# A two-layer hybrid decoder: the second mixer's small products in pairs of heads at fixed places

## The chip, the cores and the metric

The kernel runs on one core of a Trainium2 chip. The metric is device time in microseconds (us), the median of several executions; lower is better. The engines are named as the profile names them: PE multiplies matrices (PEld is its loading of the stationary operand), DVE and ACT do elementwise work, POOL fills constants, SP issues the transfers from HBM.

## What is computed

Two layers on x of 256 tokens by 1024 channels in float32, each a token mixer and a gated ConvFFN, each normed, shifted, scaled and gated by modulations of a conditioning vector c. Layer 0 has a dilated attention, layer 1 the gated linear attention (GLA) that the change touches. Cut to layer 1's mixer, and to one batch:

```python
mod = silu(c) @ w_ada[i] + b_ada[i]              # six pieces of 1024: sh1, sc1, g1, sh2, sc2, g2
h = rmsnorm(x, norm_mix[i]) * (1.0 + sc1) + sh1
...
proj = h @ w_in                                  # q, k: 4 heads of 128; v, r: 4 heads of 256; glr: 16
gk = log_sigmoid(glr @ w_gate + b_gate) / 16     # cut into chunks of 64 tokens
bcum, blast = cumsum(gk), its last row in each chunk
q_t, k_t, k_d = q * exp(bcum), k * exp(-bcum), k * exp(blast - bcum)
A = where(causal, q_t @ k_t.T, 0)                # in each chunk
kv = k_d.T @ v                                   # in each chunk
s_prev = the sum of earlier chunks' kv, decayed by exp(blast) at each step
o = A @ v + q_t @ s_prev
o = rmsnorm(o, g_norm)                           # over a head's 256 channels
x = x + g1 * ((o * silu(r)) @ w_out)
```

## The kernel before

Activations lie with channels in the partitions: x and h are eight tiles (kt) of 128 channels by 256 tokens. Each large product is made three times from split numbers (`mm3`): a weight block is loaded into `raw`, ACT casts it to `whi` (L187), DVE makes `wlo`, the rest (L191), in two halves of 1024 columns each, and PE multiplies hhi by whi (L197), hlo by whi (L198) and hhi by wlo (L199). The third product of a block therefore needs wlo's half. The pool behind `raw` has four buffers, those behind `whi` and `wlo` three each; a load starts when its buffer is free. All weight loads stand in SP's queue.

A modulation chunk (`ada_chunk`, `next_ada`) is one load of 1 MB and, on DVE, two dots of 1024 columns with silu(c) (L160). The second layer's chunks are spread over the program; the projection at the end of a mixer (`project`) needs piece 2, and the ConvFFN behind it pieces 3 to 5. `shift_columns` copies a piece into tiles that a later product reads.

The builder orders the instructions of each engine by a simulated timeline of its own. `behind(...)` puts an instruction behind others in that order; without it, the order is the simulation's.

The mixer of layer 1, in the order of the code: `h` is normed; four blocks of value weights give v; `log_gates` makes the decays e_q, e_k, e_d for all heads. Then for each head:

- `states(hd)`: large products for its query and key (tile pqk; head 0's query was made early), on DVE k_d, q_t and k_t, then small products in plain float32: two transposes of k_d (tile kdt, L995), two scores (tile a, L1001), and after a copy by ACT (kdT) and a mask by DVE (a_t) three key-value products (tiles kv and kdt, L1011), from which ACT and DVE make the states st0 to st2 (L1016, L1018).
- `output(hd)` or `products(hd)`: ten small products into tile o (L1034, L1037), then a sum of squares (osq, oacc) and its mean by PE (tile ms, L209), Ln and Exp, and two products by DVE into on (L1051).

`gate(n)` has 48 large products (tile pr) for two of r's tiles each, from weights w_r_b. Gates 0 and 1 lay the first half of wlo behind the last keys (`low=turned_keys[1:]`). Gate 2 reads copies of h's first two tiles from other addresses (lv, `level_tiles`). The calls at the end of the stage stand as `states` 0 and 1, `output` 0, `states` 2, `output` 1, `states` 3, products 2, gate 0, three modulation chunks, products 3, the norms of 2 and 3, gate 1, a chunk, gates 2 and 3; but PE takes a small product where the simulated timeline has its inputs ready, between large products of the next head.

Of the kernel before, what the change touches and what calls it, by code (L numbers as in the profile page):

```python
# [13 lines left out]
F32R = mybir.dt.float32r  # L14
# [4 lines left out]
P = 128  # L19
D = 1024  # L20
# [37 lines left out]
def trunk(ctx: ExitStack, tc: tile.TileContext, I, out):  # L58
# [396 lines left out]
    def next_ada():  # L455
        if rest:
            ada_chunk(*rest.pop(0))
# [318 lines left out]
    early = project(I["w_out_a"], lambda kt: (o_hi[kt], o_lo[kt]), 0, 0, between)  # L776
# [96 lines left out]
    def gt(shape, name, dt=F32, bufs=1, tag=None):  # L873
        return gla.tile(shape, dt, tag=tag or name, name=name, bufs=bufs)
# [8 lines left out]
    keep = gt([P, (NH_B - 1) * T], "keep", tag="D1")  # L883
# [24 lines left out]

    def gates_of(first, n, glr):
        def new(name, tag, columns=n * T):  # L910
            return gt([P, columns], name, tag=f"{tag}{min(first, 1)}")

        nz = new("nz", "A")
        for i in range(n):
# [47 lines left out]
        nc.scalar.copy(v[t][:, 0:512], pv[t][0])  # L962
        nc.vector.tensor_copy(v[t][:, 512:D], pv[t][1])

    o_n = []
    turned_keys = []

    def states(hd):
        if hd == 0:
            w = split(I["w_qk_b"][0][:, KT * P :], KT * P)  # L970
            pk = bank("pqk", "p")[:, :T]
            pq = early_q
            for kt in range(KT):
                mm3(pk, parts(w, P * kt), h[kt], kt == 0, kt == KT - 1)
        else:
            w = split(I["w_qk_b"][hd], 2048)
            pqk = bank("pqk", "p")
            pq, pk = pqk[:, :T], pqk[:, T:]
            for kt in range(KT):
                mm3(pq, parts(w, 2 * P * kt), h[kt], kt == 0, False)  # L980
                mm3(pk, parts(w, 2 * P * kt + P), h[kt], False, kt == KT - 1)
        part = min(hd, 1)
        e_q, e_k, e_d, dec = gates[part]
        own = hd - PARTS[part][0]
        c = slice(T * own, T * own + T)
        q_t, k_t, k_d = (gt([P, T], nm, bufs=2) for nm in ("q_t", "k_t", "k_d"))
        nc.vector.tensor_tensor(k_d, pk, e_d[:, c], op=ALU.mult)
        nc.vector.scalar_tensor_tensor(q_t, pq, P ** -0.5, e_q[:, c], op0=ALU.mult, op1=ALU.mult)
        last_key = nc.vector.tensor_tensor(k_t, pk, e_k[:, c], op=ALU.mult)

        ps = bank("kdt", "t")
        kd = gt([P, T], "kdT", bufs=2)
        for t in range(2):
            c = slice(P * t, P * t + P)
            nc.tensor.transpose(ps[:, c], k_d[:, c], ident)  # L995
        turned_keys[:] = nc.scalar.copy(kd, ps[:, :T]), last_key

        pa = bank("a", "s")
        for t in range(2):
            c = slice(P * t, P * t + P)  # L1000
            mm(pa[:, c], k_t[:, c], q_t[:, c], start=True, stop=True)  # L1001
        a_t = gt([P, 2, P], "a_t", bufs=2)
        nc.gpsimd.memset(a_t, 0.0)
        nc.vector.copy_predicated(a_t, causal.bitcast(U32), pa[:, :T].rearrange("p (a b) -> p a b", a=2))
        vh = slice(T * hd, T * hd + T)
        st = []
        kv = bank("kv", "s")
        for n in range(3):
            t, r = n // 2, slice(CH * (n % 2), CH * (n % 2) + CH)
            d = (kv[:, :T], ps[:, T:], kv[:, T:])[n]  # L1010
            mm(d, kd[r, P * t : P * t + P], v[t][r, vh], start=True, stop=True)  # L1011
        for n in range(3):
            d = (kv[:, :T], ps[:, T:], kv[:, T:])[n]
            s = gt([P, T], f"st{n}", bufs=2)
            if n == 0:
                nc.scalar.copy(s, d)  # L1016
            else:
                nc.vector.scalar_tensor_tensor(s, st[-1], dec[:, 4 * own + n : 4 * own + n + 1], d,  # L1018
                                               op0=ALU.mult, op1=ALU.add)
            st.append(s)  # L1020
        return q_t, a_t, st

    last_o = [None]

    def output(hd, *state):
        normed_output(hd, products(hd, *state))

    def products(hd, q_t, a_t, st):
        po = bank("o", "s")
        for et in range(2):  # L1030
            ev = slice(T * hd + P * et, T * hd + P * et + P)
            for t in range(2):
                d = po[:, T * et + P * t : T * et + P * t + P]
                mm(d, v[t][:, ev], a_t[:, t, :], start=True, stop=False)  # L1034
                for n in range(2 * t, 2 * t + 2):
                    if n:
                        last_o[0] = mm(po[:, T * et + CH * n : T * et + CH * n + CH],  # L1037
                           st[n - 1][:, P * et : P * et + P], q_t[:, CH * n : CH * n + CH],
                           start=False, stop=(n % 2 == 1))
        return po  # L1040

    def normed_output(hd, po, after=()):
        sq = gt([P, 2 * T], "osq", bufs=1)
        nc.scalar.activation(sq, po, AF.Square)
        acc = gt([P, T], "oacc", bufs=1)
        nc.vector.tensor_tensor(acc, sq[:, 0:T], sq[:, T : 2 * T], op=ALU.add)
        with behind(*after):
            rr = rstd_of([acc], 256, "s")
        on = gt([P, 2, T], f"on{hd}")
        for et in range(2):  # L1050
            nc.vector.scalar_tensor_tensor(on[:, et, :], po[:, T * et : T * et + T], col(C_GN + et), rr,  # L1051
                                           op0=ALU.mult, op1=ALU.mult)
        o_n.append(on)

    r_g = []

    def level_tiles():

        tiles = []
        for tag in ("A0", "B0", "C0", "cs0"):  # L1060
            tiles.append(gt([P, T], "lv", F32R, tag=tag))
            with behind(turned_keys[0]):
                nc.scalar.copy(tiles[-1], h[len(tiles) // 3][1 - len(tiles) % 2])
        return tiles[0:2], tiles[2:4]

    def gate(n):
        level = level_tiles() if n == 2 else ()

        w = split(I["w_r_b"][n], 2048, **({} if n else dict(after=(turned_keys[:1], ()), low=turned_keys[1:])))
        pr = bank("pr", "p")  # L1070
        for kt in range(KT):
            for s in range(2):
                with behind(*((), last_o, norm_ops[:1], ())[n]):
                    mm3(pr[:, T * s : T * s + T], parts(w, 2 * P * kt + P * s),
                        level[kt] if n == 2 and kt < 2 else h[kt], kt == 0 and s == 0, kt == KT - 1 and s == 1)
        r = gt([P, (2, 3)[n % 2] * T], f"r{n}", tag=("r0", "C1", "r2", "cs1")[n])
        r_g.append(r[:, : 2 * T].rearrange("p (a b) -> p a b", a=2))
        pr = pr.rearrange("p (a b) -> p a b", a=2)
        if n < 2:
            nc.scalar.copy(r_g[-1], pr)  # L1080
        else:
            with behind(*norm_ops[1:]):
                nc.scalar.activation(r_g[-1], pr, AF.Silu)

    s0 = states(0)
    s1 = states(1)
    output(0, *s0)
    s2 = states(2)
    output(1, *s1)
    s3 = states(3)  # L1090
    po2 = products(2, *s2)
    gate(0)
    for _ in range(3):
        next_ada()
    po3 = products(3, *s3)
    normed_output(2, po2, last_o)
    normed_output(3, po3)
    gate(1)
    next_ada()
    for n in range(4):  # L1100

        if n > 1:
            gate(n)
        r = r_g[n]
        if n < 2:
            with behind(*norm_ops[1:]):
                nc.scalar.activation(r, r, AF.Silu)
        for et in range(2):
            i = 2 * n + et
            on = o_n[n][:, et, :]  # L1110
            nc.vector.tensor_tensor(on, on, r[:, et, :], op=ALU.mult)
            hi, lo = o[i]
            last_hi = nc.scalar.copy(hi, on)
            nc.vector.tensor_tensor(lo, on, hi.bitcast(F32), op=ALU.subtract)
    exp_ln_after(last_hi)
    early = project(I["w_out_b"], o.__getitem__, 1, 0)
    gl_pool.__exit__(None, None, None)

# [147 lines left out]
```

## Time and profile before

| | us |
|---|---|
| three runs, median (lowest to highest) | 772.94 (772.45 to 775.13) |
| the profiled execution, device time | 769.98 |
| its span, first to last instruction | 768.2 |
| PE busy in the span | 756.4 |
| layer 1's mixer on PE, from its first key product to the projection's first | 63.52 |

The mixer lies from 493.27 to 556.79 us of the span, the projection from there to 578.55. A row of the timeline gives start, duration, engine, line, operation, the tiles written and read, and in brackets how long the engine stood idle before it and who ended that. PE's products overlap, so the time one takes from the others is the distance from its start to the next start. A small float32 product appears as two rows or x2.

### The profile page before, as it was taken

The page shows a single profiled execution, that of the slowest core. Times are in us where ns is not written, and L with a number is a line of the kernel's source. Part 1 is how long each engine was busy: PE and PEld are TensorE (multiplying, and loading weights), DVE is VectorE, ACT ScalarE, POOL GpSimd, SP SyncE. Part 2 cuts the span into 40 slices and gives each one's busy share as a digit, 9 for nine tenths or more (in the row PEclk, how much of TensorE's full clock was granted, in tenths as well). Part 3 has the DMA queues.
Part 4 walks back from the last instruction along what each step waited for, and adds up shares of the span by engine and source line. Part 5 has one row for each costly group of instructions (what it writes and reads, how often), then busy time and mean ns, then how long its engine had stood idle before and what let it go on. Part 6 is the DMA issues. An engine that isn't in the chain of part 4 may idle for free.

```text
span 768.2 us, 15928 instructions
## 1 busy us (share of the span) xinstructions
PE 756.4 (98%) x6420; PEld 730.1 (95%) x6420; DVE 625.2 (81%) x1120; ACT 490.3 (64%) x964; POOL 12.3 (2%) x36
## 2 busy tenths in 40 slices
PE   9999999999999999999999999999999999999997
PEld 5999989999998999999999998898999999999997
DVE  6988886878878788999988868887567998899662
ACT  5566675665666578676766456736667766666552
POOL 0000000000000010000000000000010000000100
PEclk9999999999999999999999999999999999999999
DMA  9989778587787856876656976776254756565741
GB/s 346 388 307 334 255 297 292 200 331 251 276 309 253 297 200 233 279 232 230 221 184 228 334 254 241 289 274 226 79 191 165 232 207 210 177 203 206 259 153 55
DMA packets 36487, 186.29 MB, mean 243 GB/s; under 512 B 8444, under 2 KB 11004, under 8 KB 20286
## 3 DMA queue, kind: packets, MB, share of 16 engines
q1 hardware_dynamic: 36032, 184.84, 67.4%
q8 instruction: 50, 0.82, 0.4%
q10 hardware_dynamic: 382, 0.45, 0.2%
q14 instruction: 23, 0.19, 0.1%
HBM read 184.17 MB, written 1.10 MB: 241 GB/s over the span
## 4 chain that ended last, share of the span: by engine, by line
PE 68%; DMA 13%; DVE 13%; ACT 3%; issue 2%; SPq 0%; ACTq 0%; DVEq 0%
PE pab L199 10%; PE pab L197 10%; PE pab L198 10%; DMA raw<-in_wqk 6%; PE pd L197 5%; PE pd L199 5%; PE pd L198 5%; DVE wlo L191 5%; DMA ada_raw<-in_w_ada 4%; DMA raw<-in_wv 3%; DVE ada_raw L160 3%; PE py L197 2%; PE py L198 2%; PE py L199 2%; PE pv L197 2%
## 5 line engine op out<-in xcount | busy, mean ns | idle before, releaser
L191 DVE TENSOR_TENSOR wlo<-raw,whi 128x1024 fp32r<-128x1024 f32 (+2 forms) x258 | 273.3, 1093 | 60.0 <-ACT whi L187 58.9
L187 ACT CAST whi<-raw 128x1024 fp32r<-128x1024 f32 (+2 forms) x258 | 230.5, 942 | 116.3 <-PE pab L198 40.7
L199 PE MATMUL pab<-hhi,wlo 128*128 128x256 f32 x672 | 184.7, 276 | 0.0
L198 PE MATMUL pab<-hlo,whi 128*128 128x256 f32 x672 | 184.6, 276 | 0.0
L197 PE MATMUL pab<-hhi,whi 128*128 128x256 f32 x672 | 183.2, 277 | 0.0
L198 PEld LDWEIGHTS pab<-hlo,whi 128*128 128x128 f32 x672 | 126.0, 188 | 0.2
L199 PEld LDWEIGHTS pab<-hhi,wlo 128*128 128x128 f32 x672 | 126.2, 188 | 0.0
L197 PEld LDWEIGHTS pab<-hhi,whi 128*128 128x128 f32 x672 | 125.1, 188 | 0.1
L160 DVE CUSTOM_DVE_ANT_0 ada_raw<-ada_raw,c_bc 128x1024 f32<-128x1024 f32 x96 | 113.5, 1221 | 10.3 <-DMA ada_raw<-in_w_ada 10.2
L199 PE MATMUL pd<-ghi,wlo 128*128 128x256 f32 x352 | 97.1, 276 | 0.0
L198 PE MATMUL pd<-glo,whi 128*128 128x256 f32 x352 | 97.1, 276 | 0.0
L197 PE MATMUL pd<-ghi,whi 128*128 128x256 f32 x352 | 96.8, 276 | 0.0
L197 PE MATMUL pqk<-hhi,whi 128*128 128x256 f32 x328 | 92.3, 281 | 0.1
L199 PE MATMUL pqk<-hhi,wlo 128*128 128x256 f32 x328 | 91.3, 278 | 0.0
L198 PE MATMUL pqk<-hlo,whi 128*128 128x256 f32 x328 | 91.0, 277 | 0.0
L199 PEld LDWEIGHTS pd<-ghi,wlo 128*128 128x128 f32 x352 | 66.1, 188 | 0.0
L198 PEld LDWEIGHTS pd<-glo,whi 128*128 128x128 f32 x352 | 66.1, 188 | 0.0
L197 PEld LDWEIGHTS pd<-ghi,whi 128*128 128x128 f32 x352 | 65.9, 188 | 0.0
L197 PEld LDWEIGHTS pqk<-hhi,whi 128*128 128x128 f32 x328 | 61.7, 188 | 0.7 <-issue 0.3
L199 PEld LDWEIGHTS pqk<-hhi,wlo 128*128 128x128 f32 x328 | 61.7, 188 | 0.3 <-issue 0.3
L198 PEld LDWEIGHTS pqk<-hlo,whi 128*128 128x128 f32 x328 | 61.7, 188 | 0.0
L827 ACT ACTIVATE r<-pab,small 128x256 f32<-128x256 f32 x86 | 46.7, 559 | 15.5 <-DVE r L830 15.4
(226 smaller groups left out, 1385.2 us busy)
## 6 DMA issues: line engine op xcount, KB each, us to landing
ada_raw<-in_w_ada SPq DMA_DIRECT2D x46, 1024.0 KB, 5.8
raw<-in_w_up SPq DMA_DIRECT2D x42, 1024.0 KB, 4.9
raw<-in_w_down SPq DMA_DIRECT2D x32, 704.0 KB, 5.2
raw<-in_wqk SPq DMA_DIRECT2D x18, 1024.0 KB, 7.7
raw<-in_wv SPq DMA_DIRECT2D x14, 768.0 KB, 4.6
raw<-in_w SPq DMA_DIRECT2D x6, 960.0 KB, 5.8
raw<-in_w_out_a SPq DMA_DIRECT2D x4, 1024.0 KB, 7.2
raw<-in_w_v_b SPq DMA_DIRECT2D x4, 1024.0 KB, 5.0
```

The source lines that it names most:

```text
L160: last_dot[0] = nc.vector.tensor_tensor_reduce(w, w, c_bc, op0=ALU.mult, op1=ALU.add, scale=1.0, scalar=0.0, accum_out=dot,)
L187: copied[0] = nc.scalar.copy(hi[:, c], raw[:, c])
L191: last_lo[0] = nc.vector.tensor_tensor(lo[:, c], raw[:, c], hi[:, c].bitcast(F32), op=ALU.subtract)
L197: mm(ps, a[0], b[0], start=start, stop=False)
L198: mm(ps, a[0], b[1], start=False, stop=False)
L199: return mm(ps, a[1], b[0], start=False, stop=stop)
L827: nc.scalar.activation(r, u[:, :T], AF.Identity, scale=cw[2], bias=col(C_CB + 44 * l + f))
```

## The change

The mixer works on two pairs of heads. Small products come in seven runs, and `in_turn` lays each run, and each stretch of large products, behind the one before on PE, so that the places are fixed: transposes and scores of heads 0 and 1 behind head 1's large products; key-value products of the pair behind head 2's; head 3's large products and half of gate 0 follow; transposes and scores of 2 and 3; the other half of gate 0; outputs of 0 and 1, then key-value products of 2 and 3; half of gate 1; mean square of the first pair and outputs of the second; the other half of gate 1; the second mean square; gates 2 and 3. Copies, squares, Ln and Exp are made for a pair at once, 512 columns wide. The copies lv are made ahead of the value products, and every stretch that begins behind a run reads them for tile 0 or 1 (or both). The first half of wlo stands behind head 3's last key for gate 0, and behind the last state for gate 1. Of the four modulation chunks inside the stage, two stand behind gate 1, one behind gate 3, and one in the projection, whose `shift_columns` moves behind it.

```diff
     def project(src, o_of, l, sub, between=None):
         ends = []
-        shift_columns(l, 1)
+        if between:
+            shift_columns(l, 1)
...
             if n < len(first):
                 next_ada()
+            elif n == 1:
+                with behind(last_x[0]):
+                    next_ada()
+                shift_columns(l, 1)
...
+    level = {}
+    shift(gla, 104)
+    for kt in range(2):
+        with behind(*chain[7]):
+            level[kt] = [gt([P, T], f"lv{kt}{part}", F32R) for part in range(2)]
+            for to, part in zip(level[kt], h[kt]):
+                nc.scalar.copy(to, part)
+    run = [None]
+    def in_turn(products):
+        with behind(*(run if run[0] else ())):
+            run[0] = products()
+    def keyed(hd):
...
+        nc.vector.tensor_tensor(k_d, pk, e_d[:, c], op=ALU.mult)
+        nc.vector.tensor_tensor(k_t, pk, e_k[:, c], op=ALU.mult)
+        last_key[0] = nc.vector.scalar_tensor_tensor(q_t, pq, P ** -0.5, e_q[:, c], op0=ALU.mult, op1=ALU.mult)
+    def masked(tag, *two):
...
+        in_turn(products)
+        nc.scalar.copy(kd, turned)
+    def states(first, kd):
...
+    def outputs(first, two, a_t, st):
...
+    def normed_outputs(first, po, acc):
...
+    def gate(n, between=None, **order):
+        w = split(I["w_r_b"][n], 2048, **order)
+        pr = bank("pr", "p")
+        tiles = ((0, 2, 3, 4), (1, 5, 6, 7))
...
+        in_turn(lambda: products(0))
+        if between:
+            between()
+        in_turn(lambda: products(1))
...
+    two = [keyed(0), keyed(1)]
+    kd01, a01 = masked("s", *two)
+    two.append(keyed(2))
+    st01 = states(0, kd01)
+    two.append(keyed(3))
...
+    gate(0, second_masked, low=last_key)
+    first_outputs()
+    gate(1, last_outputs, low=last_st)
+    with behind(*last_st):
+        next_ada()
+    last_on = normed_outputs(2, *late["o23"])
+    with behind(late["on01"]):
+        next_ada()
+    gate(2)
+    for n in range(2):
+        finish(n)
+    gate(3)
+    with behind(last_on):
+        next_ada()
+    finish(2)
+    exp_ln_after(finish(3))
```

Three places show how instructions move. First DVE at the keys of heads 0 and 1 (dl is a step of the decays, ISA is a dot of a modulation chunk). Before:

```order
L987 TENSOR_TENSOR k_d<-pqk,e_d 128x256
L989 TENSOR_TENSOR k_t<-pqk,e_k 128x256
L933 TENSOR_TENSOR dl<-cs 128x768
L160 ISA ada_raw,dot<-ada_raw,c_bc 128x1024
L160 ISA dot 128x1
L160 ISA ada_raw,dot<-ada_raw,c_bc 128x1024
L160 ISA dot 128x1
L191 TENSOR_TENSOR wlo<-raw,whi 128x1024 x2
L987 TENSOR_TENSOR k_d<-pqk,e_d 128x256
L988 SCALAR_TENSOR_TENSOR q_t<-pqk,e_q 128x256
L989 TENSOR_TENSOR k_t<-pqk,e_k 128x256
```

Now (keys holds k_t and k_d):

```order
L1005 TENSOR_TENSOR keys<-pqk,e_d 128x256
L1006 TENSOR_TENSOR keys<-pqk,e_k 128x256
L939 TENSOR_TENSOR dl<-cs 128x768
L191 TENSOR_TENSOR wlo<-raw,whi 128x1024 x2
L1005 TENSOR_TENSOR keys<-pqk,e_d 128x256
L1006 TENSOR_TENSOR keys<-pqk,e_k 128x256
L1007 SCALAR_TENSOR_TENSOR q_t<-pqk,e_q 128x256
```

The dots are gone from between head 0's and head 1's keys. On PE the first run now stands as below, in one piece behind the 72 large products of heads 0 and 1, where before head 1's part came 42 large products later:

```order
L199 MATMUL pqk<-hhi,wlo 128x256
L1022 MATMUL kdt<-ident,keys 128x128 x2
L1025 MATMUL a<-q_t,keys 128x128 x2
L1022 MATMUL kdt<-ident,keys 128x128 x2
L1025 MATMUL a<-q_t,keys 128x128 x2
L197 MATMUL pqk<-lv_6564,whi 128x256
L198 MATMUL pqk<-lv_6565,whi 128x256
```

Second, PE at gate 0. Before, small products stand ahead of it:

```order
L1037 MATMUL o<-q_t,st_6703 128x64
L1037 MATMUL o<-q_t,st_6705 128x64
L1011 MATMUL kdt<-v_6557,kdT 128x256
L197 MATMUL pr<-hhi,whi 128x256
L198 MATMUL pr<-hlo,whi 128x256
L199 MATMUL pr<-hhi,wlo 128x256
```

Now head 3's last large products do:

```order
L198 MATMUL pqk<-hlo,whi 128x256
L199 MATMUL pqk<-hhi,wlo 128x256
L197 MATMUL pr<-lv_6564,whi 128x256
L198 MATMUL pr<-lv_6565,whi 128x256
L199 MATMUL pr<-lv_6564,wlo 128x256
```

Third, DVE from head 3's keys to the second sum of squares now (the first wlo of the second row is gate 0's first half; the row behind st_6946 is gate 1's):

```order
L1007 SCALAR_TENSOR_TENSOR q_t<-pqk,e_q 128x256
L191 TENSOR_TENSOR wlo<-raw,whi 128x1024 x2
L1031 COPY_PREDICATED a_t<-causal,a 128x256 x2
L1081 TENSOR_TENSOR oacc<-osq 128x512
L1053 SCALAR_TENSOR_TENSOR st_6945<-st_6944,dec,kv 128x256 x2
L1053 SCALAR_TENSOR_TENSOR st_6946<-st_6945,dec,kv 128x256 x2
L191 TENSOR_TENSOR wlo<-raw,whi 128x1024
```

```order
L191 TENSOR_TENSOR wlo<-raw,whi 128x1024 x4
L1099 SCALAR_TENSOR_TENSOR on<-o,small,orstd 128x256 x4
L160 ISA ada_raw,dot<-ada_raw,c_bc 128x1024
L160 ISA dot 128x1
L160 ISA ada_raw,dot<-ada_raw,c_bc 128x1024
L160 ISA dot 128x1
L1081 TENSOR_TENSOR oacc<-osq 128x512
```

and ACT ahead of those four products on (whi is gate 3's):

```order
L168 ACTIVATE mod<-dot,one_b,small 128x1
L187 CAST whi<-raw 128x1024 x2
L1094 ACTIVATE oln<-ms,eps 128x512
L1095 ACTIVATE orstd<-oln 128x512
L1079 ACTIVATE osq<-o 128x512 x2
```

Before, the dots stood between the keys and states of all four heads, and the four sums of squares (oacc) were 256 wide, one for each head, with no dots behind head 3's keys.

More of the change, by code (lines that the diff above doesn't have):

```diff
@@ L910, in new @@
         def new(name, tag, columns=n * T):
-            return gt([P, columns], name, tag=f"{tag}{min(first, 1)}")
+            room = 4 * T if (tag, first) == ("D", 1) else columns
+            return gt([P, room], name, tag=f"{tag}{min(first, 1)}")[:, :columns]
         nz = new("nz", "A")
@@ L982, in states @@
         part = min(hd, 1)
         e_q, e_k, e_d, dec = gates[part]
-        own = hd - PARTS[part][0]
-        c = slice(T * own, T * own + T)
-        q_t, k_t, k_d = (gt([P, T], nm, bufs=2) for nm in ("q_t", "k_t", "k_d"))
+        c = slice(T * (hd - PARTS[part][0]), T * (hd - PARTS[part][0]) + T)
+        q_t = gt([P, T], "q_t", bufs=4)
+        keys = gt([P, 2 * T], "keys", bufs=2)
+        k_t, k_d = keys[:, :T], keys[:, T:]
         nc.vector.tensor_tensor(k_d, pk, e_d[:, c], op=ALU.mult)
-        nc.vector.scalar_tensor_tensor(q_t, pq, P ** -0.5, e_q[:, c], op0=ALU.mult, op1=ALU.mult)
@@ L989, in states @@
[L989 to L1053, printed above, removed]
@@ new lines, in keyed, with products @@
+        last_key[0] = nc.vector.scalar_tensor_tensor(q_t, pq, P ** -0.5, e_q[:, c], op0=ALU.mult, op1=ALU.mult)
+        return q_t, k_t, k_d
+    last_key, last_st = [None], [None]
+    def masked(tag, *two):
+        turned, pa = bank("kdt", tag), bank("a", tag)
+        kd = gt([P, 2 * T], "kdT", bufs=2)
+        a_t = [gt([P, 2, P], "a_t", bufs=4) for _ in two]
+        halves = [(i, t, slice(T * i + P * t, T * i + P * t + P)) for i in range(2) for t in range(2)]
+        for to in a_t:
+            nc.gpsimd.memset(to, 0.0)
+        def products():
+            for i, t, c in halves:
+                nc.tensor.transpose(turned[:, c], two[i][2][:, P * t : P * t + P], ident)
+            for i, t, c in halves:
+                own = slice(P * t, P * t + P)
+                last = mm(pa[:, c], two[i][1][:, own], two[i][0][:, own], start=True, stop=True)
+            return last
+        in_turn(products)
+        nc.scalar.copy(kd, turned)
+        for i in range(2):
+            nc.vector.copy_predicated(a_t[i], causal.bitcast(U32), pa[:, T * i : T * i + T].rearrange("p (a b) -> p a b", a=2))
+        return kd, a_t
@@ new lines, in states, with products @@
+    def states(first, kd):
+        kv = [bank("kv", "s") for _ in range(3)]
+        def products():
+            for i in range(2):
+                for n in range(3):
+                    t, r = n // 2, slice(CH * (n % 2), CH * (n % 2) + CH)
+                    last = mm(kv[n][:, T * i : T * i + T], kd[r, T * i + P * t : T * i + P * t + P],
+                              v[t][r, T * (first + i) : T * (first + i) + T], start=True, stop=True)
+            return last
+        in_turn(products)
+        st = [gt([P, 2 * T], f"st{n}") for n in range(3)]
+        nc.scalar.copy(st[0], kv[0])
+        for n in (1, 2):
+            for i in range(2):
+                part = min(first + i, 1)
+                at = 4 * (first + i - PARTS[part][0]) + n
+                c = slice(T * i, T * i + T)
+                last_st[0] = nc.vector.scalar_tensor_tensor(st[n][:, c], st[n - 1][:, c], gates[part][3][:, at : at + 1], kv[n][:, c],
+                                                            op0=ALU.mult, op1=ALU.add)
+        return st
@@ new lines, in trunk, with products @@
+    o_n = []
+    def normed_outputs(first, po, acc):
+        ms = bank("ms", "t")
+        def products():
+            return mm(ms, ones_d, acc.rearrange("p i t -> p (i t)"), start=True, stop=True)
+        in_turn(products)
+        ln, rr = (gt([P, 2 * T], nm, tag="kdT", bufs=2) for nm in ("oln", "orstd"))
+        nc.scalar.activation(ln, ms, AF.Ln, bias=eps[:, 0:1], scale=D / 256)
+        norm_ops[1] = nc.scalar.activation(rr, ln, AF.Exp, scale=-0.5)
+        for i in range(2):
+            on = gt([P, 2 * T], "on", tag=f"st{i}" if first else f"on{i}").rearrange("p (e t) -> p e t", e=2)
+            for et in range(2):
+                last_on = nc.vector.scalar_tensor_tensor(on[:, et, :], po[i][:, T * et : T * et + T], col(C_GN + et), rr[:, T * i : T * i + T],
+                                               op0=ALU.mult, op1=ALU.mult)
+            o_n.append(on)
+        return last_on
@@ L1083, in gate, with finish @@
                 nc.scalar.activation(r_g[-1], pr, AF.Silu)
[L1085 to L1103, printed above, removed]
+    def finish(n):
         r = r_g[n]
```

88 lines of the change are left out of this document (52 added, 36 removed).

## The prediction

> **Bound.** I read the page first, then the second layer's mixer as two windows, then PE's waits in it.
>
> ```profile
> span 768.2 us, 15928 instructions
> PE 756.4 (98%) x6420; PEld 730.1 (95%) x6420; DVE 625.2 (81%) x1120; ACT 490.3 (64%) x964; POOL 12.3 (2%) x36
> ```
>
> PE has work in 98% of the span, so time is won or lost where PE's queue stands still or where its products follow each other more slowly. The window below runs from the first key product of the mixer (493.27) to the first product of its output projection (556.79). All that the change touches on PE lies in it.
>
> ```profile
> 493.27:556.79 63.52, 62.03 (x497) 58.54 (x496) 49.77 (x86) 38.22 (x74) 0.62 (x2) 1.00 0.53 192
> ```
>
> The columns are the length, then busy time of PE, PEld, DVE, ACT and POOL, then the granted clock, the DMA share and GB/s. PE is without work for 1.49 us of 63.52, and its waits for others name nearly all of it:
>
> ```profile
> PE pr L199 <- DVE wlo L191: 0.9, 1, 0.9
> PE ms L209 <- DVE oacc L1046: 0.5, 1, 0.5
> ```
>
> So before the change PE loses 1.4 us to waits here. The small products of one head stand among the large products of another, and DVE, busy for 49.77 us, makes a key, a mask or a state while PE does something else. Whether seven fixed places give the same cover is the question.
>
> **Removed.** First, changes between small and large products.
>
> ```profile
> 501.63 0.28 PE L199 MATMUL pqk<-hhi,wlo 128*128 128x256 f32 x1
> 501.75 0.38 PE L995 MATMUL kdt<-ident,k_d 128*128 128x128 f32 x2
> 501.97 0.61 PE L1001 MATMUL a<-q_t,k_t 128*128 128x128 f32 x4
> 502.33 0.36 PE L197 MATMUL pqk<-hhi,whi 128*128 128x256 f32 x1
> 502.54 0.28 PE L198 MATMUL pqk<-hlo,whi 128*128 128x256 f32 x1
> ...
> 505.36 0.28 PE L198 MATMUL pqk<-hlo,whi 128*128 128x256 f32 x1
> 505.57 0.48 PE L1011 MATMUL kv<-v,kdT 64*128 64x256 f32 x1
> ```
>
> A large product normally follows the last after 0.12; the first one behind a run takes 0.21 (502.33 to 502.54), and the last one ahead of a run 0.12 or 0.21 (501.63, 505.36). I take 0.15 for each run. PE's order has 12 runs of small products before and 6 after (two of the seven follow each other directly), which saves 0.9 us; bounds 0.5 and 1.3. Second, the waits quoted above, 1.4 us, go from their places.
>
> Third, the pace of large products:
>
> ```profile
> 494.56 0.28 PE L199 MATMUL pqk<-hhi,wlo 128*128 128x256 f32 x1
> ...
> 545.83 0.28 PE L197 MATMUL pr<-lv,whi 128*128 128x256 f32 x1
> ...
> 547.25 0.29 PE L197 MATMUL pr<-hhi,whi 128*128 128x256 f32 x1
> ...
> 547.61 0.28 PE L197 MATMUL pr<-hhi,whi 128*128 128x256 f32 x1
> ...
> 549.99 0.28 PE L197 MATMUL pr<-hhi,whi 128*128 128x256 f32 x1
> ```
>
> From 494.56 to 501.63 there are 60 products at 0.1178 us, from 547.61 to 549.99 21 products at 0.1133. The slow pace costs 0.0045 each, and some 115 of the mixer's products have it by the same reading: 0.5 us. Products that read a level copy (lv) have 0.118 as well: 12 from 545.83 to 547.25. The change lets 90 products read copies, which costs 0.0045 x 90 = 0.4. No row shows the slow pace ended by copies, so I set the two against each other: nothing, bounds -0.5 and +0.4.
>
> **Added.** Four waits. *At the first run.* PE now transposes heads 0 and 1 in one run, behind head 1's large products, so head 1's decayed key (k_d) is needed at once.
>
> ```profile
> 501.06 1.22 DVE L160 CUSTOM_DVE_ANT_0 ada_raw<-ada_raw,c_bc 128x1024 f32<-128x1024 f32 x1
> ...
> 503.35 2.36 DVE L191 TENSOR_TENSOR wlo<-raw,whi 128x1024 fp32r<-128x1024 f32 x2
> 505.63 0.42 DVE L987 TENSOR_TENSOR k_d<-pqk,e_d 128x256 f32<-128x256 f32 x1
> 505.96 0.42 DVE L988 SCALAR_TENSOR_TENSOR q_t<-pqk,e_q 128x256 f32<-128x256 f32 x1
> 506.29 0.42 DVE L989 TENSOR_TENSOR k_t<-pqk,e_k 128x256 f32<-128x256 f32 x1
> ```
>
> The order keeps the two low halves ahead of k_d and drops the two dots of the modulation chunk: k_d moves up by 503.35 - 501.06 = 2.29, to 503.34, ends at 503.76, and the keys are all there at 504.42. PE has head 0's transposes and scores done at 502.33, waits 1.5 for k_d, takes 0.22 for two transposes, waits 0.5 for the rest. 2.0 us. Behind the waiting transposes all of PE stands. A faster pace of the 72 large products ahead would only lengthen this wait: DVE sets its end.
>
> *At gate 0.* The low half of the gate's weights (wlo, first 1024 columns) stands behind the three keys of head 3, on which PE has only just finished.
>
> ```profile
> 525.90 5.76 DVE L191 TENSOR_TENSOR wlo<-raw,whi 128x1024 fp32r<-128x1024 f32 x5
> ...
> 525.97 0.28 PE L198 MATMUL pr<-hlo,whi 128*128 128x256 f32 x1
> 527.17 0.39 PE L199 MATMUL pr<-hhi,wlo 128*128 128x256 f32 x1 [0.93 <-DVE wlo L191]
> ```
>
> Gate 0 waits so already: its third product needs wlo. Before, small products of three heads lay between head 3's large products and the gate; now nothing does. From the start of head 3's last product: 0.28 until it ends, 0.05 to DVE, three keys at a pitch of 0.33, the half at 1.2, 0.05 back: 2.6. PE gets there after 3 x 0.11. Wait: 2.3 us.
>
> *At gate 1.* Its first low half stands behind the states of heads 2 and 3, and the run ahead of it ends with their key-value products.
>
> ```profile
> 506.63 0.39 PE L199 MATMUL pqk<-hhi,wlo 128*128 128x256 f32 x1
> ...
> 534.50 0.58 ACT L1080 COPY r<-pr 128x512 f32<-128x512 f32 x1
> ...
> 536.27 0.47 DVE L1018 SCALAR_TENSOR_TENSOR st<-st,dec,kdt 128x256 f32<-128x256 f32 x1
> ```
>
> Three such products take 506.63 - 505.57 = 1.06, six 2.1. The first state needs the fourth (1.4 into the run); then a copy of 512 columns (0.58, as the row of r), four recurrences at 0.40, the half at 1.2, and 0.2 between engines: 5.0. PE gets there at 2.1 + 0.3. Wait: 2.5 us.
>
> *At the second mean square.* Call W the end of gate 1's first low half. It frees the buffer into which gate 3's weights are loaded; ACT's order has their two casts ahead of the first pair's Ln and Exp, and DVE's has four products (on) and two dots ahead of the second sum of squares (oacc).
>
> ```profile
> DMA to landing us min/median/max: 5.0/5.8/8.7
> ...
> 532.60 1.99 ACT L187 CAST whi<-raw 128x1024 fp32r<-128x1024 f32 x2 [2.72 <-PE pr L198]
> ...
> 534.98 0.48 ACT L211 ACTIVATE ln<-ms,eps 128x256 f32<-128x256 f32 x1
> ...
> 522.14 0.88 DVE L1051 SCALAR_TENSOR_TENSOR on<-o,small,rstd 128x256 f32<-128x256 f32 x2
> ```
>
> The landing row is that of the four gate loads. W + 5.0 load + 2.0 casts + 1.3 (Ln and Exp of 512 columns are not in the trace: 0.48 for 256, so between 0.5 and 0.95 each; I take 0.65) + 1.6 (four at 0.40) + 2.3 dots + 0.6 sum + 0.3 between engines = W + 13.1. PE's way there:
>
> ```profile
> 522.85 0.39 PE L1034 MATMUL o<-a_t,v 128*128 128x128 f32 x2
> ...
> 525.12 0.70 PE L1011 MATMUL kdt<-v,kdT 64*128 64x256 f32 x2
> ...
> 532.52 0.59 PE L209 MATMUL ms<-oacc,ones_d 128*128 128x256 f32 x2
> 532.95 0.61 PE L1001 MATMUL a<-q_t,k_t 128*128 128x128 f32 x4
> ```
>
> 46 large products 5.2, a mean square of 512 columns 2 x 0.43, the outputs of two heads 2 x 2.27, changes 0.3: W + 10.9. Wait: 2.2 us, between nothing (the load lands that much sooner) and 3.0 (it takes the median 5.8).
>
> Beside other work lie the rest: copies, Ln and Exp made once per pair instead of once per head save ACT about 1 us off the path (0.58 for a copy of 512 columns, where two Ln of 256 take 0.96); the four level copies stand ahead of the value products in ACT's order, long before their use; the modulation chunk moved into the projection has its dots there while PE multiplies. Loads of w_out_b slip behind gate 3's on SP's queue but keep some 10 us of lead: nothing, at most 0.5.
>
> **Sum.** As a difference: 2.0 + 2.3 + 2.5 + 2.2 - 1.4 - 0.9 = +6.7. As a whole: 360 large products at 0.1133 are 40.8; small ones are 0.9 (8 transposes at 0.11), 1.4 (8 scores at 0.18), 4.2, 9.1 and 1.7, together 17.3; six runs 0.9; waits 9.0: 68.0 against 63.52, +4.5. The first misses what the scattered order loses in trifles that no row names, the second takes the best pace everywhere. I take the middle, +5.6 us. Nothing later gives it back, because PE is never short of work behind 556.79. The profiled execution took 769.98 (span 768.2, the rest lies around it), the median of the three runs is 772.94, 3 us more; I add the difference to the median: 778.5 us.
>
> **Rivals.** *(a) Half the waits are covered*: PE comes later than I count (slow pace, trifles), or gate 3's load lands sooner. Two waits of 2.3 go, about +1.1: 774.0. For it: the two sums differ by 2. Against it: three waits are fixed chains of DVE behind PE's own last product.
>
> *(b) Faster.* DVE, rid of the eight dots (8 x 1.22) that stand ahead of gate 0 today, runs so far ahead that the lows and keys always lie ready. Then the whole-sum without waits holds, 59.0 against 63.5: 768.4. It decides at gate 0: the first low half would have to be done 2.3 us earlier. The order puts it behind keys that cannot start until PE ends, so only a small chance.
>
> *(c) The slow pace stays* through the gates and the projection: 552 products x 0.0045 = +2.5, 781.0. For it: 60 products in a row had it. Against: from 547.61 on the gates' products are fast.
>
> *(d) The clock falls in a wait.*
>
> ```profile
> 16.53 1.48 PE L644 MATMUL pqk<-hhi,whi 128*128 128x256 f32 x6
> ...
> 761.73 1.51 PE L1130 MATMUL y<-ident,x_all 128*128 128x128 f32 x12
> ...
> 766.00:768.20 2.20, 0.00 (x0) 0.00 (x0) 0.00 (x0) 0.00 (x0) 0.00 (x0) 0.50 0.36 129
> ```
>
> PE's last product ended at 763.24 and by 766.00 the granted clock was 0.50, some 2.8 us later. My waits are 2.0 to 2.5. At 16.53, six products start over about 1.28 us, 0.213 each; 24 such behind one wait cost 2.4: 780.9. [...]
>
> **Chances.** Forecast 0.58, (a) 0.22, (b) 0.06, (c) 0.07, (d) 0.07. Range 774.0 to 781.5: from (a) to one of (c) or (d), with the bounds of the load. 0.5%, about what a measurement of this kernel tells from no change, is 3.9 us: faster 0.06, same 0.22, slower 0.72.
>
> **Signs.** Right: PE's waits list k_d, wlo twice, and the second oacc, 2 us each; the mixer's window is 67 to 70 us; behind it nothing differs. Wrong: a window under 65, waits under 1 us, or a granted clock under 1.00 between.

## The result and the profile after

The changed kernel takes 779.97 us (median of 5 runs, 777.56 to 782.2), the kernel before 772.94 (5 runs, 770.96 to 775.13): a ratio of 1.0104, 95% interval 1.008 to 1.0128 (the two medians alone give 1.0091). By the medians it is slower by 7.0 us, where 5.6 was forecast. The profiled execution took 782.2. From its page, the span and the engines' busy times:

```profile
span 780.4 us, 15908 instructions
PE 760.9 (98%) x6416; PEld 733.5 (94%) x6416; DVE 624.8 (80%) x1118; ACT 488.8 (63%) x956; POOL 12.2 (2%) x36
```

The mixer as one window, from its first key product to the projection's first product (columns as in the prediction: length, PE, PEld, DVE, ACT, POOL, granted clock, DMA share, GB/s), then PE's waits in it:

```profile
498.11:568.37 70.26, 63.71 (x493) 60.22 (x492) 45.73 (x76) 34.42 (x57) 0.00 (x0) 0.95 0.46 166
```

```profile
PE pr L199 <- DVE wlo L191: 3.7, 2, 2.1
PE kdt L1022 <- DVE keys L1005: 1.4, 1, 1.4
PE kv L1041 <- ACT st L1047: 0.7, 1, 0.7
PE ms L1090 <- DVE oacc L1081: 0.5, 1, 0.5
PE a L1025 <- DVE q_t L1007: 0.2, 1, 0.2
```

The window is 6.7 us longer than before. It has 6.5 us of waits where 1.4 stood: 5.8 at the places that the prediction named, and 0.7 inside a run of key-value products (`kv`), for ACT, that it had not named. The rest of the span's growth (12.2) lies outside the mixer: it begins 4.84 later (498.11 against 493.27), and the projection, counted here to the ConvFFN's first product (582.75 before), takes 0.6 more (26.57 against 25.96). Behind that, up to PE's last product, both kernels take 180.5. The 4.84 is not the change's: PE's products ahead of the mixer are the same, and in the 13 profiles of this case the mixer begins anywhere from 492.77 to 498.62 whatever the kernel (493.24 and 498.62 for two kernels further on). So what the change does is read from the mixer and the projection.

One column differs in kind: the granted clock is 0.95 where it was 1.00. The trace's clock record has it at 0.50 in two places of the mixer, each 3.41 us long, from 509.55 and from 543.68. Windows of that length around them, and around gate 0's wait:

```profile
506.14:509.55 3.41, 1.77 (x14) 1.34 (x13) 3.41 (x6) 3.10 (x4) 0.00 (x0) 1.00 0.72 267
509.55:512.96 3.41, 3.41 (x18) 3.41 (x18) 1.60 (x3) 0.16 (x1) 0.00 (x0) 0.50 0.71 288
523.20:526.62 3.42, 1.76 (x16) 1.56 (x14) 1.85 (x4) 0.00 (x0) 0.00 (x0) 1.00 0.00 0
526.62:530.03 3.41, 2.99 (x25) 2.99 (x26) 1.50 (x2) 0.00 (x0) 0.00 (x0) 1.00 0.61 180
540.27:543.68 3.41, 1.75 (x8) 1.15 (x9) 3.10 (x6) 0.00 (x0) 0.00 (x0) 1.00 0.00 0
543.68:547.09 3.41, 3.41 (x18) 3.41 (x18) 3.41 (x6) 0.87 (x3) 0.00 (x0) 0.50 0.76 259
```

The windows at 509.55 and 543.68 hold 18 products each; at 0.1133 they would hold 30. That is 12 x 0.1133 = 1.4 us lost in each. PE was busy for 1.77 and 1.75 of the 3.41 us ahead of them; behind gate 0's window, with 1.76, the clock stayed at 1.00. So two theories stand for the tests: the added waits alone are the cost, and half-clock windows that follow from the waits are a second cost. Against both stands that something else (the copies and the pace, the moved chunks, the paired products) costs the time and the waits only show it.

### The profile page after: what moved, and what is told of

Its sections match the earlier page's. It is cut to its first block, busy times and chain, and to the rows that moved or that the text cites. A ratio compares the mean times of both kernels' runs of the same rounds, so it can differ in the third digit from the quotient of the medians.

```text
span 780.4 us, 15908 instructions
## 1 busy us (share of the span) xinstructions
PE 760.9 (98%) x6416; PEld 733.5 (94%) x6416; DVE 624.8 (80%) x1118; ACT 488.8 (63%) x956; POOL 12.2 (2%) x36
## 4 chain that ended last, share of the span: by engine, by line
PE 73%; DVE 11%; DMA 10%; ACT 3%; issue 2%; SPq 1%; ACTq 0%; DVEq 0%
PE pab L197 10%; PE pab L198 10%; PE pab L199 10%; PE pd L197 5%; PE pd L198 5%; PE pd L199 5%; DVE wlo L191 4%; DMA raw<-in_wqk 4%; DMA ada_raw<-in_w_ada 3%; DVE ada_raw L160 2%; PE pv L198 2%; DMA raw<-in_wv 2%; PE pv L197 2%; PE pv L199 2%; PE pqk L197 2%
## 5 line engine op out<-in xcount | busy, mean ns | idle before, releaser
L197 PE MATMUL pqk<-hhi,whi 128*128 128x256 f32 x314 | 88.2, 281 | 0.2 <-DVE k L556 0.2
L198 PE MATMUL pqk<-hlo,whi 128*128 128x256 f32 x314 | 86.9, 277 | 0.0
L199 PE MATMUL pqk<-hhi,wlo 128*128 128x256 f32 x314 | 86.9, 277 | 0.0
L197 PEld LDWEIGHTS pqk<-hhi,whi 128*128 128x128 f32 x314 | 59.2, 189 | 0.9 <-issue 0.5
L198 PEld LDWEIGHTS pqk<-hlo,whi 128*128 128x128 f32 x314 | 59.1, 188 | 0.0
L199 PEld LDWEIGHTS pqk<-hhi,wlo 128*128 128x128 f32 x314 | 59.0, 188 | 0.0
```

The lines of the kernel that those rows point to most:

```text
L197: mm(ps, a[0], b[0], start=start, stop=False)
L198: mm(ps, a[0], b[1], start=False, stop=False)
L199: return mm(ps, a[1], b[0], start=False, stop=stop)
```

## The experiments

Each kernel was timed against the kernel before on the same chip; ratios are to that.

**Idle time filled.** The three places get products whose results are written over.

```diff
         def products():
+            for _ in range(14 if tag == "s" else 0):
+                mm(turned[:, :T], fill[0][:, :P], level[0][0], start=True, stop=True)
             for i, t, c in halves:
...
+        def filler():
+            for _ in range(18):
+                i = mm(pr[:, :T], w[0][:, :P], level[0][0], start=True, stop=True)
+            return i
+        if n < 2:
+            in_turn(filler)
         in_turn(lambda: products(0))
```

> The changed kernel with idle PE time filled: 14 extra large products (256 columns, 1.6 us) ahead of the first run's transposes and 18 (2.0 us) ahead of each of gates 0 and 1, into banks that the next products start afresh; nothing else moves. Theory (PE standing still lets the granted clock fall): the three waits are used up, the mixer still takes 67 to 68.5 us since DVE sets its ends, but no stretch at 0.50 is left in it, the mean clock is 0.997 or more in all runs and the time is 776.5 to 778.5. Rival 1 (the clock falls by chance or by load): 0.50 stretches as often as before, 779 to 782. Rival 2 (the waits are PE's own, not DVE's): the fill comes on top, 784 to 786.

Measured: 776.91, ratio 1.0061 [1.0037, 1.0086], mean clock 0.9985 over six runs (0.9988 for the kernel before beside it). The mixer's window and two of its waits:

```profile
495.43:563.88 68.45, 65.94 (x543) 62.91 (x542) 46.43 (x78) 35.07 (x59) 0.00 (x0) 1.00 0.47 170
```

```profile
PE ms L1094 <- DVE oacc L1085: 1.6, 1, 1.6
PE a L1029 <- DVE q_t L1009: 0.2, 1, 0.2
```

Fifty more products in the window and 1.8 us less. The ends of the three waits are DVE's, PE's extra work fits into them but for a few tenths, and no half-clock window is left in the mixer (its clock is 1.00). At full clock the change costs the mixer at most 68.45 - 63.52 = 4.9 us. Rivals 1 and 2 fall. The fourth wait is 1.6 here, where the changed kernel's profile has 0.5: there the half-clock window from 543.68 brought PE later to a sum of squares that came no later. DVE's rows, the changed kernel first: gate 1's first low half, then the second sum of squares.

```profile
542.16 1.22 DVE L191 TENSOR_TENSOR wlo<-raw,whi 128x1024 fp32r<-128x1024 f32 x1
...
555.62 0.69 DVE L1081 TENSOR_TENSOR oacc<-osq 128x512 f32<-128x512 f32 x1
```

```profile
537.89 1.22 DVE L191 TENSOR_TENSOR wlo<-raw,whi 128x1024 fp32r<-128x1024 f32 x1
...
551.13 0.68 DVE L1085 TENSOR_TENSOR oacc<-osq 128x512 f32<-128x512 f32 x1
```

From the end of the one to the end of the other: 556.31 - 543.38 = 12.9, and 551.81 - 539.11 = 12.7. The chain is the same, so that half-clock window cost the changed kernel little beyond what the fourth wait would have taken anyway.

**The low halves freed.**

```diff
-    gate(0, second_masked, low=last_key)
+    gate(0, second_masked)
     first_outputs()
-    gate(1, last_outputs, low=last_st)
+    gate(1, last_outputs)
```

> The changed kernel without the two orders on the first low halves of gates 0 and 1 (behind head 3's last key, behind the last state); the builder's timeline places them. Theory: the waits at both gates (2.1 and 1.6 us in the changed kernel's trace) go, and the half-clock stretch behind the second with them, while the wait for the first run's keys stays at 1.4 to 2: 774 to 776, ratio to the kernel before 1.001 to 1.004, mixer 64 to 66. Rival (the low halves are 1.1 us each on DVE wherever they stand): keys or states are late by as much, a wait for keys or kdT takes the place, 779 to 781.

Measured: 771.54, ratio 0.9996 [0.9978, 1.0013]: no loss can be told any more, which is more than expected. The mixer, and PE's waits in it:

```profile
493.24:556.87 63.63, 61.26 (x494) 58.38 (x492) 45.13 (x74) 34.38 (x57) 0.00 (x0) 0.97 0.52 181
```

```profile
PE kdt L1022 <- DVE keys L1005: 1.4, 1, 1.4
PE kv L1041 <- ACT st L1047: 0.7, 1, 0.7
PE a L1025 <- DVE q_t L1007: 0.2, 1, 0.2
```

Both waits on wlo are gone and nothing takes their place; keys and states are not later. The fourth wait went too, which I hadn't expected: gate 1's first low half ends earlier, frees its buffer earlier, and gate 3's weights with all that hangs on them come earlier. The one wait of 1.6 that is left (1.4 and 0.2, at the first run) has a half-clock window behind it in this profile as well (from 505.39, by the clock record). One of the two orders is older than the change: the kernel before lays gate 0's first low half behind head 3's last key too, and waits 0.9 there. At gate 1 it has none, contrary to what the section on it says (in `gate(n)` the order is for n = 0 alone). What freeing gate 0's half would give the kernel before was not run.

**The first run one head later.**

```diff
     two = [keyed(0), keyed(1)]
-    kd01, a01 = masked("s", *two)
     two.append(keyed(2))
-    st01 = states(0, kd01)
+    kd01, a01 = masked("s", *two[:2])
     two.append(keyed(3))
+    st01 = states(0, kd01)
```

> The changed kernel with the first run (transposes and scores of heads 0 and 1) moved behind head 2's large products and the pair's key-value products behind head 3's. Theory: 48 large products (5.5 us) now cover the keys of head 1, the wait of 1.6 goes and the half-clock stretch behind it (some 1.5): 776.5 to 778.5, mixer 66 to 68; the low-half waits at the gates stay, the first maybe covered by the six key-value products (2.1 us) that now stand ahead of gate 0, then 775. Rival (DVE is the bound of this stretch, the wait moves to the next thing that DVE makes): 779.5 to 781.

Measured: 774.0, ratio 1.0023 [1.0005, 1.0041]. Window and waits:

```profile
497.99:562.28 64.29, 61.63 (x494) 58.57 (x492) 45.59 (x76) 34.31 (x57) 0.00 (x0) 0.97 0.52 184
```

```profile
PE pr L199 <- DVE wlo L191: 1.7, 1, 1.7
PE kv L1041 <- ACT st L1047: 0.7, 1, 0.7
PE ms L1090 <- DVE oacc L1081: 0.3, 1, 0.3
```

Two waits go with this edit: the keys' behind 48 large products, and gate 0's behind the six key-value products that now stand ahead of it. The window is shorter than expected, though gate 1's wait still has a half-clock window behind it (from 538.48, hence the 0.97).

**No level copies** (the loop that makes them taken out).

> The changed kernel without the level copies: every large product reads h itself. Theory (copies and their pace are worth nothing here, DVE's waits set the time): 779 to 781, mixer within 0.6 of 70.3. Rival 1 (a run of small products leaves a slow pace of 0.1178 which the copies end): 0.0045 for each of some 280 large products behind the first run, +1.3: 781 to 783. Rival 2 (the products that read copies are the slow ones): 90 times 0.0045, -0.4, not to be told from nothing in the time, but to be seen in the pace.

Measured: 779.45, ratio 1.0097 [1.0074, 1.012], mixer:

```profile
498.62:568.13 69.51, 63.59 (x493) 59.99 (x492) 45.40 (x75) 34.48 (x57) 0.00 (x0) 0.95 0.48 168
```

No difference in the time can be told, as expected where DVE sets the ends; the mixer is 0.75 shorter than with copies, just outside the 0.6 expected. In the pace there is a difference: counted by the distance from start to start (slow from 0.1155 to 0.123), 247 of the mixer's large products are slow and 81 fast; with the copies 107 and 210. The others are first or last ones of a run, or at half clock.

**Both edits together, with and without the copies.**

> Both edits in one: low halves of gates 0 and 1 placed by the timeline, and the first run one head later. Theory (the waits on DVE were all that the fixed places cost, and without them what the change removes is left): no wait over 0.8 in the mixer, no half-clock stretch in it, mixer 61 to 62.5 against 63.5 before the change, time 769.5 to 771.2, ratio 0.996 to 0.998. Rival (the supply of weights is the next bound: the projection's second tile waited 0.9 for its cast where only the low halves were freed): that wait grows to 2 or 3, 771.5 to 773.

> The same without the level copies, now that no DVE wait sets the ends. Theory 1 (a run of small products leaves the slow pace, which copies end): some 280 large products behind the first run at 0.1178 instead of 0.1133, +1.0 to +1.3 beside the run with copies. Theory 2 (the pace does not hang on the copies): within 0.3 of it in the mixer's window.

Measured: 770.82, ratio 0.9976 [0.9959, 0.9993], and 771.53, ratio 0.9981 [0.9959, 1.0002]. The mixer with the copies and without:

```profile
492.77:552.73 59.96, 59.25 (x494) 56.79 (x492) 45.10 (x74) 34.30 (x57) 0.00 (x0) 1.00 0.55 192
```

```profile
497.18:557.83 60.65, 59.94 (x493) 57.47 (x492) 45.37 (x75) 34.27 (x57) 0.00 (x0) 1.00 0.55 190
```

The mixer falls to 59.96, 3.6 under the kernel before and below what was expected, yet the time falls by 1.2 only. The paired products, the moved chunks and, in one of the two kernels, the copies are all still there; so the loss was not theirs, it lay in the orders and the place of the first run. The copies are worth 0.7 in the window (104 slow products against 298, 194 x 0.0045 = 0.9) in one profile each, between the two theories; the timed runs don't separate the two kernels. What is missing is in the projection: it takes 27.98 in the kernel with copies, 25.96 before the change. There PE's second product waits 0.9, as it did with the low halves freed alone; the rival's 2 or 3 did not come:

```profile
553.91 0.39 PE L197 MATMUL py<-ohi,whi 128*128 128x256 f32 x1 [0.91 <-ACT whi L187]
```

and 189 of its products have the slow pace in this profile, 0.9 more; one of the kernel without copies has it fast, so that part doesn't hang on the edit alone, and why is open.

**The projection's third block held.** The waiting product belongs to the third weight block; the builder had put its first product ahead of its cast.

```diff
-                with behind(*(ends[n - 2 :][:1] if (n, kt) == (2, 2) else ())):
+                with behind(*(ends[n - 2 :][:1] if n == 2 and kt in ((2,) if between else (0, 2)) else ())):
```

> The two edits together, and the projection's third weight block held behind the end of its first on PE: before, its first product stood second in the projection, ahead of its own cast, and PE waited 0.9 there. Theory (that place alone, not the supply of weights, costs the 0.9): the wait goes or shrinks to 0.3 or 0.5 (the products then follow the casts of o), 0.4 to 0.9 below the kernel without the hold: 769.8 to 770.6, projection 26 to 27.2. Rival (the casts are late because of the loads, which stand behind modulation chunks): the wait comes back some products later, no difference, 770.8.

Measured: 768.18 (9 runs, 765.75 to 769.7) against 771.48, ratio 0.9955 [0.9934, 0.9975]: the lowest time of all and under the 769.8 to 770.6 expected. Its span and all of PE's waits in mixer and projection:

```profile
span 766.4 us, 15909 instructions
```

```profile
PE kv L1041 <- ACT st L1047: 0.7, 1, 0.7
PE py L198 <- DVE olo L1142: 0.3, 1, 0.3
```

The wait shrinks to 0.3 as expected, and the projection takes 26.54. The rest of the 1.4 us against 27.98 is pace: nearly all of its products are fast here. Behind the projection this execution took 182.2 instead of 180.5, with 376 slow products where the kernel without the hold had 29, so its span (766.4) is no shorter than that kernel's (766.1). The intervals of the two ratios overlap; that the two edits and the hold together beat the kernel before is shown, what the hold alone is worth in time is not.

**Half the filling** (7, 9 and 9 products).

> As the filled kernel, with half the extra products (7, 9 and 9): waits of 0.8 to 1.3 us stay at the three places. [...]

Measured: 780.66, ratio 1.0102 [1.0076, 1.0128], mean clock 0.9953. PE's waits, then windows at the three half-filled places, and the only half-clock window of this mixer with the one ahead of it:

```profile
PE ms L1094 <- DVE oacc L1085: 1.8, 1, 1.8
PE pr L199 <- DVE wlo L191: 1.6, 2, 1.0
...
PE kdt L1026 <- DVE keys L1007: 0.6, 1, 0.6
```

```profile
507.05:510.47 3.42, 2.61 (x21) 2.18 (x20) 3.22 (x6) 2.47 (x3) 0.00 (x0) 1.00 0.69 213
524.12:527.53 3.41, 2.41 (x20) 2.41 (x21) 2.08 (x2) 0.00 (x0) 0.00 (x0) 1.00 0.41 111
541.18:544.60 3.42, 3.14 (x24) 2.90 (x25) 3.42 (x6) 0.87 (x3) 0.00 (x0) 1.00 0.63 192
551.14:554.55 3.41, 1.61 (x13) 1.38 (x12) 3.41 (x7) 2.21 (x4) 0.00 (x0) 1.00 0.75 296
554.55:557.96 3.41, 3.41 (x13) 2.51 (x12) 2.42 (x4) 2.69 (x6) 0.00 (x0) 0.50 1.05 346
```

At the three half-filled places the clock is 1.00, and behind them too (PE busy for 2.61, 2.41 and 3.14 us of the three windows); the 0.50 comes behind the fourth wait, which I had left out of the expectation, with 1.61 busy ahead of it. At gate 1 there are two short waits (0.7 for the state's bank, then 0.6 for wlo; the 1.0 above is gate 0's); what the clock did there in the five runs that have no trace isn't shown. This run leaves an open end: against its own kernel before it is 8.6 slower, as much as the changed kernel, though its mean clock (0.9953 against 0.994) leaves room for fewer half-clock windows.

**A longer wait at gate 0.**

```diff
+    spare = gt([P, 4 * T], "spare", tag="D1")
+    with behind(*last_key):
+        for _ in range(2):
+            held = nc.vector.tensor_copy(spare, v[0])
-    gate(0, second_masked, low=last_key)
+    gate(0, second_masked, low=[held])
```

> The changed kernel with two copies of 1024 columns by DVE (1.2 us each, read by nobody) ahead of gate 0's low half: its wait grows from 2.1 to 4.4 or 4.8. [...] Rival (the clock does not go by PE's idle time): the copies alone, 782 to 782.5, and no stretch at this place.

Measured: 783.13, ratio 1.0138 [1.0108, 1.0167], mean clock 0.991, none of the six runs over 0.993. The two copies took 0.7 us each and not 1.2, so the wait grew to 3.4 only:

```profile
519.14 1.41 DVE L1166 COPY spare<-v 128x1024 f32<-128x1024 f32 x2
```

```profile
PE pr L199 <- DVE wlo L191: 5.1, 2, 3.4
```

The windows at gate 0:

```profile
517.49:520.90 3.41, 0.84 (x8) 0.63 (x6) 2.73 (x6) 0.00 (x0) 0.00 (x0) 1.00 0.00 0
520.90:524.31 3.41, 2.58 (x12) 2.58 (x13) 1.92 (x2) 0.00 (x0) 0.00 (x0) 0.50 0.46 115
524.31:527.73 3.42, 3.42 (x18) 3.42 (x18) 0.00 (x0) 0.95 (x1) 0.00 (x0) 0.50 0.46 192
```

The window that lies in the wait, with PE busy for 0.84 of 3.41 us, is followed by two at half clock. By the rival the copies alone would add 1.3; against its own kernel before the run is 11.1 slower, the changed kernel 7.0 and, in the last experiment below, 8.8; that is 2.3 to 4.1 more, so more than the copies.

**The filled kernel with one chunk later.**

```diff
-    with behind(*last_st):
-        next_ada()
     last_on = normed_outputs(2, *late["o23"])
-    with behind(late["on01"]):
+    with behind(norm_ops[1]):
+        next_ada()
+    with behind(last_on):
         next_ada()
```

> The filled kernel (no half-clock stretch at the first three waits) with the first modulation chunk behind gate 1 moved behind the second mean square. Theory (the fourth wait is DVE's dots and ACT's casts ahead of the second sum of squares, 1.6 in the filled kernel): it goes, mixer 66.3 to 67.2. Whether the time falls with it: 775.3 if nothing follows; rival (the chunk's load and dots now collide with the projection's weights and casts, what is won is given back at its first products): 776.5 to 777.5, with waits of 1 to 2 us in the projection.

Measured: 777.05, ratio 1.0079 [1.0053, 1.0106]. Window, and waits from there into the projection:

```profile
493.00:559.61 66.61, 65.69 (x544) 62.85 (x542) 42.99 (x71) 34.09 (x57) 0.00 (x0) 1.00 0.44 158
```

```profile
PE py L198 <- DVE olo L1153: 0.7, 1, 0.7
PE py L197 <- ACT r L1141: 0.6, 1, 0.6
PE py L197 <- ACT whi L187: 0.5, 1, 0.5
```

The edit moves both chunks of gate 1, and the trace has no dot ahead of the second oacc there. The fourth wait is gone and the mixer 1.8 shorter, but the projection takes 29.43 where the filled kernel has 25.96: 1.8 of it are three waits at its first products, as the rival had it, and 187 of its products have the slow pace, 0.8. What ended the fourth wait was DVE's and ACT's work ahead of oacc; moving the chunks only moved where PE waits.

**The changed kernel again.**

> The changed kernel once more, with no edit, beside the others on one chip. 779 to 781, clock 0.992 to 0.998. Theory (the clock is granted by windows of 3.41 us whose edges lie elsewhere in each execution): the half-clock stretches stand at other waits than in the first profile, or in other number, and the time follows their number at some 1.5 us each; the waits of 1.6, 2.1 and 1.6 stay where they are, and the fourth is 1.6 to 1.9 if no stretch lies ahead of it behind gate 1, about 0.5 if one does.

Measured: 780.25 (6 runs, 778.72 to 784.58) against 771.48, ratio 1.0126 [1.0097, 1.0155], clock 0.991 to 0.995. So beside its own kernel before it is 8.8 slower here, and was 7.0 at first. Windows cut at the edges of this execution's clock record:

```profile
504.73:508.14 3.41, 1.77 (x13) 1.34 (x13) 3.41 (x6) 2.61 (x4) 0.00 (x0) 1.00 0.70 219
508.14:511.55 3.41, 3.41 (x18) 3.41 (x17) 0.88 (x3) 0.00 (x0) 0.00 (x0) 0.50 0.64 267
521.80:525.21 3.41, 1.33 (x11) 1.13 (x10) 2.50 (x5) 0.00 (x0) 0.00 (x0) 1.00 0.00 0
525.21:528.62 3.41, 3.41 (x17) 3.41 (x17) 0.86 (x1) 0.00 (x0) 0.00 (x0) 0.50 0.75 257
538.87:542.28 3.41, 1.67 (x8) 0.97 (x6) 2.69 (x6) 0.59 (x1) 0.00 (x0) 1.00 0.00 0
542.28:545.69 3.41, 2.76 (x13) 2.77 (x14) 3.41 (x6) 0.87 (x3) 0.00 (x0) 0.50 0.53 149
```

Now all three waits have a half-clock window behind them, gate 0's too; the first three waits are as long as in the first profile, and the fourth does not appear among PE's waits at all. The mixer takes 72.39.

## Why the prediction was right, and where it was wrong

The direction, the mechanism and the range held. That the number came near is in part luck. The prediction had two sums for the mixer, +6.7 and +4.5, and took their middle, +5.6. The mixer shows at most +4.9 at full clock, so the second sum was the good one and the middle too high; the clock, which both left out, added some 3 us by the estimate under rival (d).

- **Bound.** Right for this change: every edit that took a DVE wait from PE shortened the mixer. Where DVE set the ends, more work for PE (the fill) or a slower pace (no copies) did not lengthen it; with the waits gone, the slower pace did, by 0.7.
- **Removed.** Too small in the first sum. It was put at 0.9 + 1.4 = 2.3. With both edits the mixer takes 59.96, and 59.0 without the wait inside the key-value run (1.0 from start to start): 63.52 - 59.0 = 4.5 were removed. From start to start these are waits 1.6, changes and pace of the large products 0.8, and 2.1 in the small products themselves (18.6 before, 16.5 now), which the first sum had only as "trifles that no row names". The second sum had 59.0 for the same whole; its small products (17.3) were put too high and its large ones with their changes (41.7, measured 42.4) too low by as much.
- **Pace.** The step "No row shows the slow pace ended by copies, so I set the two against each other: nothing" failed in its reading: with copies the slow stretches are short (107 slow products, 247 without), worth 0.7 where no wait follows. That a faster pace ahead of a wait gives nothing was right.
- **Four waits.** Nearly right. The prediction counted them from start to start, while the lists above have only idle time, without the end of the product ahead of the wait. From start to start, less the usual 0.11, they were 2.0, 2.2 and 1.8 in the changed kernel's first profile, and 1.75 at the fourth place in the filled kernel: 7.8, where 2.0, 2.3, 2.5 and 2.2, together 9.0, were predicted. The wait inside the key-value run, 1.0 by the same count, was not named and makes most of that up. The chain behind the fourth wait was sized well: 13.1 predicted, 12.7 to 12.9 measured.
- **Later parts.** For this change nearly right: 0.6 in the projection, where at most 0.5 was named, and nothing behind it. It holds only as long as the mixer waits: with the waits gone, the projection gave 2.0 back.
- **Rival (d).** This is the step that failed: (d) had a chance of 0.07. Half-clock windows came behind the waits in both profiles of the changed kernel, two and three times. What they cost over all runs is an estimate: the mean clock of its 11 runs is 0.994, that of the filled kernel 0.9985; one window of 3.41 us at half clock lowers the mean by 0.0022, so some 2 more windows for each run, 1.4 us each by the 12 products lost, 2.8 (the prediction's 2.4 was for 24 slow products; the two half-clock windows of the first profile's mixer hold 18 each). The times agree roughly: beside its own kernel before, the changed kernel is 7.0 and 8.8 slower, the filled one 4.3, so 2.7 to 4.5 are left for the clock. The half-filled kernel does not fit so well, and the price of one window stays uncertain. "A granted clock under 1.00 between" was named as a sign of being wrong, and it came; the window (70.26) is just over the 67 to 70 named as right.
- **Rivals (a), (b), (c).** No wait was covered, so (a) fell. (b) fell for this change, and it fell at gate 0's low half, as said; with the lows free and the first run later the mixer had its 59. The time did not follow in full: with the projection's hold it is 3.3 under its own kernel before, where (b) had 4.5 (that 768.18 stands so near to (b)'s 768.4 is chance: the kernel before had 772.94 at first and 771.48 here). (c) fell for this profile: in its projection 7 products are slow.

## What to carry to other kernels

A small product at a fixed place needs as much independent work between it and the last input of its operands as the chain on the other engines is long, counted with what stands ahead of that chain in the queue; ordering a weight's low half behind such a chain puts it on the path as well. To see what a wait costs beyond itself, fill it with products that are written over: if the time falls although the ends stay, as here (ratio 1.0061 against 1.0104, mean clock 0.9985 against 0.994), the clock was part of the price. Half a fill told nothing here. And look for what is won in the next stage: here 2.0 of 3.6 us were given back by one product placed ahead of its cast and by pace.

## What the runs showed of the hardware

In the changed kernel's first profile, up to PE's last product, the granted clock is 0.50 in three stretches of 3.41 us, from 157.98, 509.55 and 543.68. They begin 351.57 and 34.13 apart, 103 and 10 times 3.413. In the second profile it is 0.50 in the mixer from 508.14, 525.21 and 542.28, which is 17.07 apart each, 5 times 3.414; the last of the three lasts two windows, to 549.11. 509.55 - 508.14 = 1.41 is no multiple of 3.41, so the beginnings lie elsewhere in the second execution. The same wait met them differently: gate 0's 2.1 us had the clock at 1.00 behind it in the first and at 0.50 in the second.

PE's busy time in a window of 3.41 us does not by itself tell the clock of the next one in these profiles. Behind 0.84 us (the longer wait), 1.33 (the second profile, gate 0) and 1.61 (half the filling) the clock was 0.50, and behind 2.41 and 2.61 (half the filling) it was 1.00. In the first profile it was 0.50 behind 1.75 and 1.77, but 1.00 behind 1.76 and behind 1.70, in these rows:

```profile
246.72:250.14 3.42, 1.70 (x11) 1.38 (x10) 1.81 (x4) 2.92 (x7) 0.00 (x0) 1.00 0.95 381
250.14:253.55 3.41, 3.41 (x60) 2.67 (x60) 3.41 (x5) 3.13 (x5) 0.00 (x0) 1.00 0.48 130
```

At half clock, 2.58 and 2.76 busy (from 520.90 with the longer wait, from 542.28 in the second profile) were followed by another window at 0.50, and 3.41 (from 509.55 and from 543.68 in the first) by 1.00. What sets the clock is not shown.

The large products of the mixer follow each other, at full clock, mostly at one of two distances in these profiles, 0.1133 and 0.118, and one distance can hold for tens of products in a row: in the profile before, 72 slow ones from 493.27 and 81 fast ones from 547.61. In the changed kernel's first profile the longest slow stretch has 21 products (from 527.26); without copies the mixer begins with 72 (498.62 to 507.10). But the copies are not all that ends one: in the profile before, 41 fast products follow from 527.75, ahead of the mixer's first read of a copy at 545.83. What begins the slow pace is not shown.
